# A hybrid decoder block on one core: the diagonal spread in half 0's group norms, row sums on 64 columns, and one value-gate projection moved ahead of v

## The chip, the cores and the metric

The kernel runs on one core of one Trainium2 chip, as one program with one launch. The metric is the device time in microseconds. A core has TensorE (PE, with its weight loads shown as PEld), VectorE (DVE), ScalarE (ACT), GpSimd (POOL) and SyncE (SP), which here issues the DMAs. Each engine works through its own list of instructions in order and waits on semaphores for the others.

## What is computed

One decoder block on x of 1024 tokens by 1024 features, all float32. The tokens are processed in two halves of 512, "half 0" and "half 1".

```python
cond = silu(c) @ ada_w + ada_b                       # shift1, scale1, gate1, shift2, scale2, gate2
h = rmsnorm(x, norm1_g) * (1 + scale1) + shift1
u, v, val, gate = split(h @ w_in + b_in, 4 x 512)    # in order u, v, val, gate
# branch a: causal spatial gating inside chunks of 128 tokens, 8 heads of 64
v = layernorm(gelu(v), a_ln_g, a_ln_b)
y_a = gelu(u) * (tril(w_s) @ v + b_s)
# branch b: gated, causal depthwise convolution of width 31, group norm on 8 groups of 64, swish
y_b = val * sigmoid(gate)
y_b = silu(groupnorm(conv31(y_b) + conv_b))
y = concat(rmsnorm(y_a, out_norm_a_g), rmsnorm(y_b, out_norm_b_g))
x = x + gate1 * (y @ w_out)
h2 = rmsnorm(x, norm2_g) * (1 + scale2) + shift2
g, up = split(h2 @ w_ffn_in, 2)                      # 2 x 2816
x = x + gate2 * ((silu(g) * up) @ w_ffn_out)
return rmsnorm(x, norm_f_g) * (1 + scale_f) + shift_f
```

## The kernel before

Activations lie with features on the 128 partitions and the 512 tokens of a half along the free dimension. So a matrix product is a chain of matmuls of 128 by 128 weights with 512 moving columns into one PSUM bank. To keep float32 accuracy from the rounded format fp32r, each operand is split into a high part (a cast on ScalarE) and a low part (a subtraction on GpSimd or VectorE), and each product is three matmuls: high by high, low by high, high by low (`mm3`, L682 to L684; `product`, L1073).

The block is written as a sequence of stages: first projection of half 0 (value and gate, eight banks at once), `u_proj` of both halves, `v_proj`, `conv`, `spatial`, `a_out` and `b_out`, the value-gate projection of half 1 (`vg_proj(1, ...)`), `w_out`, then the second norm and the feed-forward part. In the feed-forward part twelve "ahead" tiles (`ah`, L1073) are computed before half 1's output projection, eight more after it, and the rest uses a fast product scheme with seven products in place of eight.

The convolution runs on VectorE: 31 taps, each a multiply-add of a shifted row of `ypad` into a PSUM bank `cv` (L1006, L1009, L1011). Of half 0's taps the first six go to ScalarE (L1000) and GpSimd (L1001). Tiles come in pairs (`conv_pair`), and each pair is followed by `group_norm`, which centres two tiles with one matmul each (L1026), squares them (L1029, L1030), sums over groups of 64 partitions in 32-column matmuls (L1033) and forms one 128 by 128 tile of reciprocal standard deviations `gsd` (L1036, L1037). The rows of that tile are then spread back over the partitions of both tiles. There are two ways of doing it:

- by block: 16 matmuls in plain float32 with 64 stationary columns and 128 moving columns, one for each tile, quarter of the tokens and group (L1046). Half 0's group norms do it so.
- from the diagonal: `diagonal` writes the four blocks of 32 rows on the diagonal of a 128 by 512 tile of zeros, each row as a high and a low part (a cast on ScalarE, L617, and four VectorE instructions, L620), and one fp32r matmul for each tile against the selector `late["picks"]` spreads it (L1042). Half 1's group norms and several RMS norms do it so (the set `DIAGONAL`); for these the tile `late` is set up once (`load_late`, L610 to L612), in a buffer that holds the spatial weights `wt` before.

The result is multiplied onto the tile (L1049) and goes through Silu (L1050). `b_out` squares and sums all four tiles (L720, L724, L727), spreads the RMS scale (L730 to L737) and writes `yn_b` (L962) and the high and low parts `y_b` (L964, L965), on which `w_out` (L682 to L684, banks `po`) waits.

`spatial_bias` (L789 to L794) sums each head's causal spatial weights over the source tokens, to carry the layer norm's shift into the bias `bst`: two float32 matmuls of ones with 128 stationary columns and 512 moving ones, and eight VectorE updates of 64 partitions by 128. `v_proj` makes v by tokens, 128 at a time, with Gelu (L910), statistics (L912, L913) and normalisation on VectorE (L921). `glu` writes value times sigmoid of gate into `ypad` (L756, L758).

What is not on the main path is queued as `background`: 24 sums for the conditioning vectors (`ada_cols`) each load 512 KB and multiply and add on VectorE (L636), or on GpSimd and ScalarE (L633, L634); one is issued with each weight or token tile.

The order that runs is not the written order. At the end `fix_order` takes the list of all instructions with their dependencies, estimates durations, computes how long the work behind each instruction is, and lays out each engine's list from that, in several rounds. What the written order does bind is the buffers: tiles of one tag are handed out in the order of the program. The tags that matter here: `w` (eight tiles, the high and low parts of four weights), `raw` (four tiles of 512 KB for loads), `mm` (three PSUM banks), `cv` and `gn` (two banks each), `vn` (four).

## Time and profile before

| | us |
| --- | --- |
| three runs | 966.22, 967.76, 967.87 |
| median | 967.76 |
| the profiled execution, its own time | 967.97 |
| its span (first to last instruction) | 965.9 |
| mean granted TensorE clock | 0.995 of full speed |

The busy times of all engines are on the profile's page, of which the prediction quotes the lines it uses. All rows are of the one profiled execution; times in them count from the start of its span. Rows of a timeline begin with the start and the duration. Float32 matmuls appear as two records for each instruction, fp32r matmuls as one. Consecutive records of TensorE overlap, so what one costs is the distance from its start to the next start.

### The profile page before, as it was taken

How to read it: one execution, taken by the hardware profiler on the slowest of the kernel's cores; microseconds unless marked ns; L12 is line 12 of the kernel's file. 1: busy time of each engine (PE TensorE's matmuls, PEld its weight loads, DVE VectorE, ACT ScalarE, POOL GpSimd, SP SyncE). 2: the span in 40 equal slices, each digit the busy share in tenths (PEclk: the TensorE clock that was granted, in tenths of full speed). 3: DMA queues.
4: the chain of work that ended last, by engine and by line, in shares of the span. 5: the costliest groups of instructions: out<-in, count | busy, mean ns of one | idle time of the engine just before them, and what ended most of it. 6: DMA issues, size and time to landing. Idle time of an engine off the chain costs nothing.

```text
span 965.9 us, 12960 instructions
## 1 busy us (share of the span) xinstructions
PE 950.5 (98%) x4521; PEld 769.6 (80%) x4521; DVE 871.7 (90%) x1236; ACT 474.0 (49%) x756; POOL 408.6 (42%) x241
## 2 busy tenths in 40 slices
PE   8999999999999999999999999999999999999996
PEld 4887777778777778788888888888888888888885
DVE  6999999999999763999999999999879999969956
ACT  5787477643474753564333333333337437227426
POOL 0089988836453413665444444455433100000132
PEclk9999999999999999999999999999999999999998
DMA  9882542343485444844677678867657857415104
GB/s 353 323 310 91 176 152 69 113 174 131 137 282 188 158 136 146 271 173 147 215 245 239 230 237 261 268 211 257 211 177 264 266 172 258 162 33 159 61 1 174
DMA packets 70498, 184.24 MB, mean 191 GB/s; under 512 B 7841, under 2 KB 8353, under 8 KB 70434
## 3 DMA queue, kind: packets, MB, share of 16 engines
q1 hardware_dynamic: 70434, 183.43, 56.5%
q8 instruction: 35, 0.57, 0.2%
q14 instruction: 29, 0.24, 0.1%
HBM read 142.24 MB, written 41.16 MB: 190 GB/s over the span
## 4 chain that ended last, share of the span: by engine, by line
PE 79%; DVE 15%; ACT 2%; DMA 2%; issue 1%; SPq 0%; ACTq 0%; DVEq 0%
PE B L1073 30%; PE C L1073 18%; PE ah L1073 10%; DVE cv L1006 5%; PE A L1073 3%; PE v L682 2%; PE v L684 2%; PE po L682 2%; PE po L684 2%; PE v L683 2%; PE po L683 2%; PE p L684 1%; PE p L683 1%; PE p L682 1%; DVE ada L636 1%
## 5 line engine op out<-in xcount | busy, mean ns | idle before, releaser
L1073 PE MATMUL B<-h,w_f 128*128 128x512 f32 x816 | 189.6, 389 | 0.1
L1073 PEld LDWEIGHTS B<-h,w_f 128*128 128x128 f32 x816 | 153.0, 188 | 32.5 <-ACT x L1291 0.8
L1006 DVE SCALAR_TENSOR_TENSOR cv<-ypad,colt,cv 128x512 f32<-128x512 f32 x216 | 147.0, 744 | 0.2
L1073 PE MATMUL B<-fa,w_d 128*128 128x512 f32 x528 | 124.8, 389 | 0.1
L1073 PE MATMUL C<-h,w_f 128*128 128x512 f32 x528 | 123.4, 389 | 0.0
L1073 PEld LDWEIGHTS B<-fa,w_d 128*128 128x128 f32 x528 | 98.8, 188 | 21.4 <-DVE x L1433 0.7
L1073 PEld LDWEIGHTS C<-h,w_f 128*128 128x128 f32 x528 | 99.1, 188 | 20.6
L1073 PE MATMUL ah<-h,wh_a 128*128 128x512 f32 x320 | 102.4, 396 | 0.3 <-ACT h L699 0.3
L1359 POOL TENSOR_TENSOR sq_nf<-sq_nf,sq_nf 128x512 f32<-128x512 f32 (+1 forms) x15 | 18.0, 1202 | 170.2 <-ACT sq_nf L1353 170.0
L666 POOL TENSOR_TENSOR wl_a<-raw_a,wh_a 128x1024 fp32r<-128x1024 f32 x20 | 49.8, 2488 | 78.2 <-ACT wh_a L665 78.2
L1065 ACT ACTIVATE w_d<-raw_d 128x512 fp32r<-128x512 f32 (+1 forms) x72 | 42.0, 593 | 80.9 <-PE B L1073 32.6
L1065 ACT ACTIVATE w_f<-raw_f 128x512 fp32r<-128x512 f32 x68 | 42.5, 629 | 75.9 <-PE B L1073 41.5
L1316 POOL TENSOR_TENSOR x<-x,up 128x512 f32<-128x512 f32 x20 | 33.2, 1659 | 105.6 <-ACT x L1315 105.6
L1066 DVE TENSOR_TENSOR w_f<-raw_f,w_f 128x512 fp32r<-128x512 f32 x68 | 70.2, 1039 | 2.6 <-ACT w_f L1065 2.5
L1073 PEld LDWEIGHTS ah<-h,wh_a 128*128 128x128 f32 x320 | 60.0, 188 | 15.7 <-ACT h L699 1.4
L1073 PE MATMUL C<-fa,w_d 128*128 128x512 f32 (+1 forms) x291 | 63.9, 370 | 0.0
L1073 PE MATMUL ah<-h,wl_a 128*128 128x512 f32 x160 | 62.5, 390 | 0.0
L1073 PEld LDWEIGHTS C<-fa,w_d 128*128 128x128 f32 x291 | 51.0, 188 | 9.2
L1066 DVE TENSOR_TENSOR fa<-a,fa 128x512 fp32r<-128x512 f32 x77 | 52.4, 720 | 0.4 <-ACT fa L1065 0.4
L1433 DVE SCALAR_TENSOR_TENSOR x<-B,cond,x 128x512 f32<-128x512 f32 x48 | 35.6, 745 | 18.2 <-PE B L1073 18.0
L1066 DVE TENSOR_TENSOR w_d<-raw_d,w_d 128x512 fp32r<-128x512 f32 (+1 forms) x72 | 49.1, 691 | 1.1 <-ACT w_d L1065 1.1
L1065 ACT ACTIVATE fa<-a 128x512 fp32r<-128x512 f32 x77 | 46.1, 625 | 7.1 <-DMA a<-acts 4.0
(265 smaller groups left out, 2111.2 us busy)
## 6 DMA issues: line engine op xcount, KB each, us to landing
acts<-x SPq DMA_DIRECT2D x77, 256.0 KB, 2.9
a<-acts SPq DMA_DIRECT2D x77, 256.0 KB, 4.0
raw_f<-wf SPq DMA_DIRECT2D x32, 512.0 KB, 4.0
ada<-ada SPq DMA_DIRECT2D x24, 512.0 KB, 3.5
x<-ada SPq DMA_DIRECT2D x24, 512.0 KB, 4.4
raw_a<-wf SPq DMA_DIRECT2D x20, 512.0 KB, 3.9
ahead<-ahead SPq DMA_DIRECT2D x40, 256.0 KB, 2.6
ypad<-ada SPq DMA_DIRECT2D x16, 512.0 KB, 5.7
```

What stands on the lines that cost most here:

```text
L636: V.scalar_tensor_tensor(raw, raw, 1.0, cact, op0=ALU.mult, op1=ALU.mult, accum_out=cond[:, j:j + 1])
L666: lo_eng.tensor_tensor(lo[:, cut], raw[:, cut], hi[:, cut].bitcast(F32), op=ALU.subtract)
L682: PE.matmul(acc, shi, mhi, start=start, stop=False)
L683: PE.matmul(acc, slo, mhi, start=False, stop=False)
L684: PE.matmul(acc, shi, mlo, start=False, stop=stop)
L1006: V.scalar_tensor_tensor(accs[j], src, wc, accs[j], op0=ALU.mult, op1=ALU.add)
L1065: A.activation(dst[:, 0, :], src, AF.Copy)
L1066: lo_eng.tensor_tensor(dst[:, 1, :], src, dst[:, 0, :].bitcast(F32), op=ALU.subtract)
L1073: last_mm = PE.matmul(bank[:, cols], s, m[:, cols], start=first and p == 0 and i == 0, stop=p == n - 1 and i == 2, skip_group_check=True)
L1316: G.tensor_tensor(g0, g0, up0, op=ALU.mult)
L1359: G.tensor_tensor(run, run, t, op=ALU.add)
L1433: V.scalar_tensor_tensor(x_tile(k, part), bank[:, cols], ccol(GATE2, k), x_tile(k, part), op0=ALU.mult, op1=ALU.add)
```

## The change

Three things change in the kernel, and a constant tile on the host is built to suit.

1. In `group_norm`, the group norms that are not in `DIAGONAL` (half 0's two) take a fresh tile of 128 by 1024 from the tag `raw`: GpSimd clears its first half, ScalarE widens four columns of a constant into a 128 by 256 selector, and `diagonal` builds the diagonal in it. The 16 float32 matmuls become two of fp32r.
2. `spatial_bias` uses 64 stationary columns: one matmul for the even heads into partitions 0 to 63 and one for the odd heads into 64 to 127 of a single bank, and four VectorE updates on all 128 partitions.
3. `vg_proj(1, (0,))` is written ahead of `v_proj(0)`; tiles 1 and 2 stay where all three were.

```diff
     ("out_norm_a_g", 4), ("out_norm_b_g", 4), ("b_conv_w", 4 * CW),
-    ("sel_grp", 16), ("low_rows", 1), ("sel_hl", 1),
+    ("picks", 4), ("low_rows", 1), ("sel_hl", 1),
...
-    def diagonal(src):
-
-        diag, low = late["diag"], late["low"]
+    def diagonal(src, diag=None, low=None):
+
+        if diag is None:
+            diag, low = late["diag"], late["low"]
         A.activation(low, src, AF.Copy)
...
     def spatial_bias():
-        for q in range(2):
-            rs = mm_bank(f"rs{q}")
-            PE.matmul(rs, ones.broadcast_to([P, P]), wt[:, 4 * q:4 * q + 4, :], start=True, stop=True)
-            for hh in range(4):
-                hd = 4 * q + hh
-                e, hp = hd % 2, hd // 2
-                rows = slice(e * 64, (e + 1) * 64)
-                V.scalar_tensor_tensor(bst[rows, hp, :], rs[rows, hh * P:(hh + 1) * P],
-                                       col("a_ln_b", hp)[rows], bst[rows, hp, :],
-                                       op0=ALU.mult, op1=ALU.add)
+        rs = mm_bank("rs")
+        heads = wt.rearrange("p (a e) t -> p e a t", e=2)
+        for e in range(2):
+            PE.matmul(rs[e * 64:(e + 1) * 64], ones.broadcast_to([P, 64]), heads[:, e], start=True, stop=True)
+        for hp in range(4):
+            V.scalar_tensor_tensor(bst[:, hp, :], rs[:, hp * P:(hp + 1) * P], col("a_ln_b", hp), bst[:, hp, :],
+                                   op0=ALU.mult, op1=ALU.add)
...
         by_block = f"g{half}{jp}" not in DIAGONAL
-        both = sd if by_block else diagonal(sd)
+        picks = None
+        if by_block:
+            both = sb.tile([P, 2 * H], F32R, tag="raw", name=f"gd{half}{jp}", bufs=N_RAW)
+            diag, work = both[:, 0:H], both[:, H:]
+            G.memset(diag.bitcast(F32), 0.0)
+            picks = work[:, P:3 * P]
+            A.activation(picks.rearrange("p (a b) -> p a b", a=4), colt[:, _OFF["picks"]:_OFF["picks"] + 4].unsqueeze(2).broadcast_to([P, 4, 64]), AF.Copy)
+            both = diagonal(sd, diag, work[:, 0:P])
+        else:
+            picks, both = late["picks"], diagonal(sd)
         for i, (j, b) in enumerate(zip(js, (b1, b0))):
-            if not by_block:
-                PE.matmul(b, late["picks"][:, i * P:(i + 1) * P], both, start=True, stop=True)
-            for q in range(4):
-                for g in range(2):
-                    if by_block:
-                        PE.matmul(b[g * 64:(g + 1) * 64, q * P:(q + 1) * P],
-                                  col("sel_grp", 8 * i + 2 * q + g).broadcast_to([P, 64]), sd,
-                                  start=True, stop=True)
+            PE.matmul(b, picks[:, i * P:(i + 1) * P], both, start=True, stop=True)
...
     background += [lambda i=i: ada_cols(SHIFT2 * 8 + i, pool=i < 12) for i in range(16)]
+    vg_proj(1, (0,))
     v_proj(0)
...
-    vg_proj(1, (0, 1, 2))
+    vg_proj(1, (1, 2))
     w_out(0, ya0 + yb0)
```

More of the change, by code (lines that the diff above doesn't have):

```diff
@@ L1536 @@
     gind = np.zeros((P, 34))
-    sel_grp = np.zeros((P, 2, 4, 2))
+    heads = np.zeros((P, 2, 2))
     picks = np.zeros((P, 2 * P + 1))
@@ L1542 @@
             picks[2 * i + g::16, i * P + 64 * g:i * P + 64 * g + 64] = 1.0
-            for q in range(4):
-                sel_grp[32 * q + 2 * i + g, i, q, g] = 1.0
+            heads[2 * i + g::16, i, g] = 1.0
     picks[0::16, 2 * P] = 1.0
-    colv.update(sel_grp=sel_grp.reshape(P, 16),
+    colv.update(picks=heads.reshape(P, 4),
                 low_rows=-(part[:, None] // 16 % 2), sel_hl=((part == 0) | (part == 32))[:, None])
```

## The prediction

> **What bounds the kernel now.** I read the page's first two parts, TensorE's own waits, a table of stages, and then the timelines of single engines around the places that the change touches.
>
> ```profile
> PE 950.5 (98%) x4521; PEld 769.6 (80%) x4521; DVE 871.7 (90%) x1236; ACT 474.0 (49%) x756; POOL 408.6 (42%) x241
> PE   8999999999999999999999999999999999999996
> DVE  6999999999999763999999999999879999969956
> PEclk9999999999999999999999999999999999999998
> ```
>
> TensorE is busy in every slice at the full granted clock, but so is VectorE in the first third. Busy is not the same as never waiting, so next come TensorE's waits between 60 and 400 us (its line, what it waited for, us in total, times, longest):
>
> ```profile
> PE ssq_n L737 <- DVE rt_n L731: 1.0, 1, 1.0
> PE ah L1073 <- ACT h L699: 0.3, 1, 0.3
> PE gn L1026 <- DVE s L1049: 0.2, 1, 0.2
> PE ssq_n L733 <- DVE late L620: 0.2, 1, 0.2
> ```
>
> That is 1.7 us in 340. TensorE is the bound: a microsecond of matmuls taken out is a microsecond of span, as long as what TensorE needs next is also there a microsecond earlier. Whether it is there is VectorE's matter. The table of stages gives the length, then busy us of PE, PEld, DVE, ACT and POOL:
>
> ```profile
> 61.00:212.00 151.00, 150.04 (x863) 118.54 (x862) 150.27 (x218) 100.40 (x150) 123.50 (x70) 1.00 0.43 142
> 266.00:317.00 51.00, 50.68 (x236) 39.61 (x235) 50.61 (x80) 29.17 (x46) 25.28 (x12) 1.00 0.68 233
> 317.00:349.00 32.00, 31.73 (x152) 23.78 (x150) 20.71 (x32) 23.08 (x35) 9.91 (x7) 1.00 0.43 148
> 349.00:966.00 617.00, 607.83 (x2742) 502.24 (x2740) 543.87 (x746) 258.35 (x435) 211.07 (x127) 0.99 0.58 192
> ```
>
> In the two stages up to 317 us VectorE idles 0.7 and 0.4 us: it is as full as TensorE. It first has room from 317 to 349, where 11.3 us are idle. Two engines are full at once, and the change has to be priced on both.
>
> **TensorE: what goes.** The group of the old spread, and rows of TensorE's timeline (start, duration):
>
> ```profile
> L1046 PE MATMUL gn<-gsd,colt x64: 272/273/323, 144.4 to 177.9; 128*64 128x128 f32 x64
> 107.63 1.88 PE L789 MATMUL rs<-wt,ones 128*128 128x512 f32 x4
> 109.29 0.50 PE L682 MATMUL v<-wh_v,h 128*128 128x512 f32 x1
> 144.38 1.97 PE L1046 MATMUL gn<-gsd,colt 128*64 128x128 f32 x32
> 146.28 0.50 PE L684 MATMUL v<-wl_v,h 128*128 128x512 f32 x1
> 319.90 0.39 PE L1042 MATMUL gn<-late 128*128 128x512 f32 x1
> 320.13 0.39 PE L1073 MATMUL ah<-h,wh_a 128*128 128x512 f32 x1
> ```
>
> I count from one start to the next, because the durations overlap. For half 0's first group norm 32 records take 146.28 - 144.38 = 1.90 us; there are 64, so 3.80. Half 1 already spreads from the diagonal: 320.13 - 319.90 = 0.23 for one matmul. Half 0 would need four, 0.92. Saved: 2.9. The full-width matmul behind the narrow block shows 0.50 where others show 0.39, so some 0.1 more for each group norm: 0.2. The row sums: 109.29 - 107.63 = 1.66 us for two matmuls with 128 columns. For 64 columns L1046 is the nearest form: 32 records are 16 matmuls over 128 moving columns in 1.90 us, 0.119 each; two over 512 are eight of those, 0.95. Saved 0.7; the ends are 0 (a narrow one costs as much as a wide one) and 0.83 (exactly half). TensorE's sum: 2.9 + 0.2 + 0.7 = **3.8 us less**, between 3.1 and 3.9.
>
> The Trainium skill (TensorEngine Tiling (Array Packing), section Overview) allows up to twice the speed where the stationary side has 64 columns or fewer. By that rule the row sums would save 0.83 and the sum would be 3.9; the L1046 row stays a little short of it.
>
> **The other engines: what comes.** Rows of their timelines, and one line's group with its shortest, median and longest duration in ns:
>
> ```profile
> 112.51 2.91 DVE L794 SCALAR_TENSOR_TENSOR bst<-rs,colt,bst 64x128 f32<-64x128 f32 x8
> 115.45 2.73 DVE L1006 SCALAR_TENSOR_TENSOR cv<-ypad,colt,cv 128x512 f32<-128x512 f32 x4
> 316.66 1.41 DVE L620 SCALAR_TENSOR_TENSOR late<-late,colt,gsd 32x128 fp32r<-32x128 f32 x4
> 318.10 2.72 DVE L962 SCALAR_TENSOR_TENSOR yn_a<-ya,colt,ssq_a 128x512 f32<-128x512 f32 x4
> 330.22 1.30 POOL L724 TENSOR_TENSOR sq_b<-sq_b,sq_b 128x512 f32<-128x512 f32 x1 [4.60 <-ACT sq_b L720]
> 330.37 2.37 DVE L620 SCALAR_TENSOR_TENSOR late<-late,colt,gsd 32x128 fp32r<-32x128 f32 x4 [0.23 <-ACT late L617]
> 207.24 0.41 ACT L611 ACTIVATE late<-picks_raw 128x257 fp32r<-128x257 f32 x1
> 316.20 0.31 ACT L617 ACTIVATE late<-gsd 128x128 fp32r<-128x128 f32 x1 [1.76 <-DVE gsd L1037]
> 188.61 0.52 POOL L612 MEMSET late<- 128x512 f32 x1
> L921 DVE TENSOR_SCALAR vn<-vn,mv,sd x8: 541/1512/2620, 141.3 to 176.8; 128x512 f32<-128x512 f32 x8
> ```
>
> The bias update falls from eight instructions to four of the same 128 columns on twice the partitions. Eight take 115.45 - 112.51 = 2.94 us, so 1.47 goes; if partitions cost time, less, down to nothing. Each diagonal adds four pieces on VectorE: 318.10 - 316.66 = 1.44 us undisturbed, 2.37 in the other place, where a GpSimd addition ran beside the first piece. Two diagonals are 2.9 to 4.7; I take 2.9, the undisturbed row, as GpSimd is met or not by chance. VectorE's sum: 2.9 - 1.5 = **1.4 us more**, between 1.4 and 4.7.
>
> ScalarE gets for each group norm a cast of the reciprocal (0.31) and the widening of the selector (256 columns; the copy of 257 took 0.41): 1.4 us in all, hidden because ScalarE is busy 100.4 of 151 us in that stage. GpSimd gets two clearings of 0.52, in a stage with 27.5 us idle. In the chain of a group norm, cast and diagonal put 0.31 + 1.44 between reciprocal and spread: the diagonal waits on VectorE, with conv taps (L1006) queued behind it, and the spread waits on TensorE, with the v or value-gate matmuls behind it. Both queues are laid out by the planner, which can put such work ahead, so I cost these waits at nothing; uncovered, they would cost 1.75 us twice.
>
> **What is moved.** The value-gate projection is 48 matmuls, 48 x 0.23 = 11 us of TensorE, the same work in another place: its own price is zero, and half 0's v, its normalisation and spatial mixing come 11 us later. What does that meet? Rows of VectorE, TensorE and ScalarE, and the page's row for the loads of the conditioning sums (KB of one, median us from issue to landing):
>
> ```profile
> 192.73 3.34 DVE L636 SCALAR_TENSOR_TENSOR ada<-ada,cact 128x1024 f32<-128x1024 f32 x1
> 206.45 3.06 DVE L965 TENSOR_TENSOR y_b<-yn_b,y_b 128x512 fp32r<-128x512 f32 x3
> 212.41 0.39 PE L682 MATMUL po<-y_b,wh_o 128*128 128x512 f32 x1
> ada<-ada SPq DMA_DIRECT2D x24, 512.0 KB, 3.5
> 185.56 1.28 ACT L756 ACT_TABLE_LOAD   x1
> ```
>
> Half 0's first normalised conv tile is there at 206.45 + 3.06 / 3 = 207.5, TensorE reads it first at 212.41: 4.9 us to spare, of which the 3.8 faster TensorE and the 1.4 heavier VectorE take 5.2. But ahead of it VectorE does work that is not yet due, such as the reduction of 3.34 us at 192.73, and v's normalisation now comes behind more of conv half 0 than before. I cost this place at nothing. Weights: the projection's four tiles (two weights, high and low) now stand between u's eight and v's eight in a ring of eight, so v's last tiles wait for the projection instead of for u. Today's handover, with v's first matmul at 109.29 right behind the row sums, shows no stall in the waits above; but the row sums, 1.66 us of cover, shrink to 0.95, and if the other 0.7 is bare it costs 0.7. ScalarE's Sigmoid now falls between two runs of Gelu: one or two more table loads of 1.28 us, hidden as above. On SyncE's queue the two weight loads go ahead of v's, and the reductions' loads they carry come earlier; the two diagonals each hold one of four load buffers until their spread.
>
> **Where it ends.** The hard meeting point is half 1's conv branch:
>
> ```profile
> 281.50 0.62 ACT L1030 ACTIVATE s<-gn 128x512 f32<-128x512 f32 x1
> 316.08 0.68 DVE L1006 SCALAR_TENSOR_TENSOR cv<-ypad,colt,cv 128x512 f32<-128x512 f32 x1
> 316.79 0.60 ACT L1017 ACTIVATE s<-cv 128x512 f32<-128x512 f32 x1 [0.28 <-DVE cv L1006]
> 322.08 1.13 PE L1026 MATMUL gn<-s,cstt 128*128 128x512 f32 x2 [0.20 <-DVE s L1049]
> 348.32 1.95 ACT L964 ACTIVATE y_b<-yn_b 128x512 fp32r<-128x512 f32 x3 [3.89 <-DVE yn_b L962]
> 349.10 0.41 PE L682 MATMUL po<-y_b,wh_o 128*128 128x512 f32 x1
> ```
>
> VectorE ends its last conv tap at 316.76 and the copy is done at 317.39. The next matmul on it (L1026) starts only at 322.08, since both banks were still held by the other group norm of half 1: 4.7 us that are no work. From there the chain goes straight on to the first half 1 tile, written from 348.32 to about 348.97, and TensorE reads it at 349.10. Nothing to spare. And TensorE has nothing else then: the same twelve ahead tiles and three banks fill it up to here in both kernels.
>
> So if VectorE ends its taps L us later than now, and the 4.7 us wait can shrink to nothing, the span changes by the larger of -3.8 and L - 4.7. With L = 1.4: L - 4.7 = -3.3. The other group norm of half 1 is ready early enough for that, as its values were copied by 282.12 (the row at 281.50); it was merely put late, in step with TensorE, and with TensorE 3.8 us ahead it moves up by as much: 322.08 - 3.8 = 318.3, beside 317.39 + 1.4 = 318.8. The profiled execution took 967.97 us (span 965.9), 0.21 above the median of 967.76. 967.97 - 3.3 = 964.7, or **964.5** against the median.
>
> **The rivals.** What a measurement of this kernel can tell from no change is about 0.2%, 1.9 us.
>
> First: the wait before L1026 stays 4.7 us, because the planner puts the first group norm of half 1 in step with VectorE's taps, not with TensorE. Then the tap's delay passes through: TensorE waits 3.8 + 1.4 and the span gains 1.4, 969.2. For it: VectorE is as full as TensorE up to 317. Against: the wait is idle time that any earlier place of two short matmuls removes. It reads as no change.
>
> Second, the slower side: the normalisation of v (L921), 11 us later, meets more of GpSimd's work, and so do the diagonals. The eight instructions of L921 run from 0.54 to 2.62 us at one shape, half of them up to 1.51, and the row at 330.37 shows a diagonal stretched by 0.93 beside GpSimd's 1.30. GpSimd is busy 123.5 of 151 us there. If the middle of the eight goes from 1.51 to 2.07, halfway to the longest, that is 8 x 0.56 = 4.5 us; with both diagonals stretched, 1.8 more: L = 1.4 + 6.3 = 7.7, so +3.0, or 970.8 against the median. It decides from L = 6.6 on, where L - 4.7 passes 1.9. Against: they may as well meet less of it, for GpSimd's additions for the conv fall elsewhere too.
>
> The Trainium skill (SBUF — State Buffer, the sections on the port pair that the two engines share) says that a VectorE instruction with two SBUF inputs and a GpSimd one that reads SBUF exclude each other for the whole instruction. The diagonal's pieces are of that kind, and the stretched row agrees.
>
> Third: a diagonal, cleared early, holds a load buffer for long, and a weight arrives late. A load takes 3.5 us from issue to landing (the row above), and one such stall on top of -3.3 gives +0.2, no change: 968.0. Against it: GpSimd can clear late, in 0.52 us.
>
> Fourth, that the order asked for is not the order run: the planner sorts by its own times, and only the order of buffers binds it. That changes no term of the sum, only L.
>
> **How the numbers follow.** The forecast (TensorE's gain less what L eats, so L below 2.8): 0.54. The first rival 0.18, the second 0.22, the third 0.06. Faster by over 0.2% is the forecast: 0.54. Within 0.2%: the first and third rivals, 0.24. Slower: 0.22. The range begins at 963.4 (967.76 - 3.9, and 0.5 for waits of TensorE's 1.7 that may close) and reaches to 970.4, through the first and third rivals and into the second, up to just short of its price. The dearer part of the second rival (0.14) and a forecast that gains more than priced (0.04) lie outside.
>
> **What would show it.** Right: TensorE's records for the spread in half 0 are four of full width, 0.23 from start to start; the row sums take about 0.95; TensorE's waits from 60 to 400 us stay under 3 us; L1026 of half 1's second group norm follows its copy within 2 us; VectorE's last tap ends at 317 to 319. Wrong: a wait of TensorE on y_b or yn_b in half 1, or on h of the second norm, of over 2 us; the last tap beyond 323; L921 with a mean near 2 us; a wait on a weight tile after the moved projection.

## The result, and the profile after

The changed kernel takes 971.86 us (median of 16 runs, 967.26 to 974.14) against 967.38 for the kernel before (16 runs, 965.72 to 968.66): ratio 1.0041 (95% interval 1.0029 to 1.0052). It is slower by 0.4%; the forecast was 964.5.

Line numbers after the change are one or two off those before: L1048 is the spread, L791 the row sums, L919 the normalisation of v, L621 the diagonal's pieces, L1004 a conv tap, L637 a conditioning sum, L738 an RMS spread. Two executions of it are shown below: its profiled one (968.79 us, span 967.0), which is one of its quick ones, and the profiled one of e1, the same kernel once more (span 970.0, nearer to the median).

The page's busy times, first execution:

```profile
PE 947.2 (98%) x4460; PEld 766.2 (79%) x4461; DVE 876.3 (91%) x1240; ACT 474.0 (49%) x760; POOL 409.9 (42%) x243
```

TensorE's work fell by 3.3 us (950.5 before), VectorE's rose by 4.6. Rows of TensorE's timeline (start, duration):

```profile
107.95 1.08 PE L791 MATMUL rs<-wt,ones 128*64 128x512 f32 x4
108.96 0.50 PE L683 MATMUL p<-h,wh_vg 128*128 128x512 f32 x1
157.92 0.62 PE L1048 MATMUL gn<-gd 128*128 128x512 f32 x2
158.38 0.39 PE L684 MATMUL v<-wh_v,h 128*128 128x512 f32 x1
```

The row sums take 1.01 from start to start, the spread 0.23 for each matmul: what was priced. Then TensorE's waits from 60 to 400 us (line, what it waited for, us in total, times, longest), first execution, then e1:

```profile
PE pu L683 <- ACT sg L757: 1.0, 1, 1.0
PE ssq_a L738 <- DVE rt_a L732: 0.9, 1, 0.9
PE po L683 <- ACT y_b L962: 0.9, 1, 0.9
PE gn L1048 <- DVE late L621: 0.8, 1, 0.8
PE gn L1048 <- DVE gd L621: 0.5, 1, 0.5
PE ah L1073 <- DVE ahead L1090: 0.4, 1, 0.4
PE ssq_n L734 <- DVE late L621: 0.2, 1, 0.2
```

```profile
PE pm L945 <- DVE s L1049: 1.7, 1, 1.7
PE ssq_b L738 <- DVE rt_b L732: 1.4, 1, 1.4
```

The kernel before had 1.7 us of waits here. Now there are 4.7 in the quick execution and 7.6 in e1 (these two lines come on top of nearly the same list). The stage tables (length, busy us of PE, PEld, DVE, ACT, POOL), first execution, then the first stage of e1:

```profile
61.00:212.00 151.00, 148.67 (x808) 117.04 (x809) 149.60 (x218) 101.93 (x154) 125.56 (x72) 1.00 0.42 140
266.00:317.00 51.00, 51.00 (x240) 40.54 (x239) 50.56 (x80) 27.19 (x42) 27.60 (x13) 1.00 0.68 218
317.00:349.00 32.00, 30.21 (x141) 21.46 (x139) 26.01 (x38) 22.72 (x35) 9.96 (x7) 1.00 0.36 123
```

```profile
61.00:212.00 151.00, 147.04 (x799) 115.49 (x799) 149.28 (x211) 102.00 (x154) 124.66 (x72) 1.00 0.41 137
```

VectorE is as full as before up to 317 us, and from 317 to 349 it works 26.0 us where it worked 20.7. TensorE now stands still in e1 for 4.0 of these 151 us; before it was 1.0.

For all later comparisons I cut each profiled execution in four by TensorE's timeline: the start of u (first `pu`), from there to the end of half 0's w_out (start of the last `po` of half 0), from there to the first matmul on half 1's `y_b`, and the rest.

| execution | start of u | to the end of w_out, half 0 | to y_b, half 1 | rest | sum |
| --- | --- | --- | --- | --- | --- |
| before | 60.74 | 192.23 | 96.12 | 616.75 | 965.84 |
| after, quick | 61.92 | 189.38 | 97.98 | 617.69 | 966.97 |
| after, e1 | 61.92 | 192.82 | 97.96 | 617.26 | 969.95 |

In the second stage the quick execution does gain 2.85 us, and e1 loses 0.6: the stage is not the same length each time. In the third both lose 1.9. The start is later by 1.2 and the rest longer by 0.5 to 0.9, though nothing in the source was changed there; in e5 and e6, with the same order, u starts at 60.63 and 63.57, so the start varies from one execution to the next.

### The profile page after: what moved, and what is told of

The parts are those of the page before. It is cut to its first block, busy times and chain, and to the rows that moved or that the text cites. A ratio compares the mean times of both kernels' runs of the same rounds, so it can differ in the third digit from the quotient of the medians.

```text
span 967.0 us, 12841 instructions
## 1 busy us (share of the span) xinstructions
PE 947.2 (98%) x4460; PEld 766.2 (79%) x4461; DVE 876.3 (91%) x1240; ACT 474.0 (49%) x760; POOL 409.9 (42%) x243
## 4 chain that ended last, share of the span: by engine, by line
PE 85%; DVE 10%; ACT 2%; DMA 2%; issue 1%; SPq 0%; POOL 0%; ACTq 0%; DVEq 0%; POOLq 0%
PE B L1073 29%; PE C L1073 17%; PE ah L1073 8%; PE A L1073 3%; PE po L683 3%; PE po L685 3%; PE po L684 3%; PE p L683 2%; PE p L685 2%; PE p L684 2%; PE pu L683 2%; PE pu L685 2%; PE pu L684 2%; DVE cv L1004 1%; PE v L685 1%; PE v L684 1%
## 5 line engine op out<-in xcount | busy, mean ns | idle before, releaser
L1004 DVE SCALAR_TENSOR_TENSOR cv<-ypad,colt,cv 128x512 f32<-128x512 f32 x216 | 146.8, 742 | 0.1
```

The lines of the kernel that those rows point to most:

```text
L1004: V.scalar_tensor_tensor(accs[j], src, wc, accs[j], op0=ALU.mult, op1=ALU.add)
```

## The experiments

Times are medians; ratios are against the kernel before on the same chip, with the 95% interval.

### Once more, and each part alone

e1 is the changed kernel, no edit.

> The changed kernel again, for a second profile and a second set of times. All theories: 967 to 974 us as before, median near 971.9, wider than the 3 us of the kernel before. Port theory (VectorE's diagonal pieces collide with GpSimd's conv additions): the last conv tap of half 1 ends at 322 us or later, and a longer execution shows it later still, with TensorE's wait on y_b longer. Plan theory (the order dealt anew leaves TensorE short waits in many places, each decided by how transfers and engines happen to meet): a longer execution shows its extra microseconds in several places, also behind 400 us, in the feed-forward part.

971.9 us, 1.004 (1.0027 to 1.0052). Its third stage is as long as in the quick execution; the second differs by 3.4. Up to 187.5 us the two executions run alike, but for one row at 76.5, and then these rows differ, first of the quick execution and then of e1 (VectorE's last normalisation of v, GpSimd's low part of a weight):

```profile
187.58 0.55 DVE L919 TENSOR_SCALAR vn<-vn,mv,sd 128x512 f32<-128x512 f32 x1
187.72 2.67 POOL L667 TENSOR_TENSOR wl_o<-raw_o,wh_o 128x1024 fp32r<-128x1024 f32 x1 [3.48 <-ACT wh_o L666]
```

```profile
187.56 2.75 DVE L919 TENSOR_SCALAR vn<-vn,mv,sd 128x512 f32<-128x512 f32 x1
187.63 2.39 POOL L667 TENSOR_TENSOR wl_o<-raw_o,wh_o 128x1024 fp32r<-128x1024 f32 x1 [3.40 <-ACT wh_o L666]
```

VectorE's row begins ahead of GpSimd's in both, by 0.14 us in the quick execution, where it takes 0.55, and by 0.07 in e1, where it takes 2.75 and ends 0.29 behind GpSimd's. In e5 and e6 (below, the same order) the lead is 0.01 and 0.09, and it takes 2.69 and 2.76. What follows on VectorE is 2.2 us later in e1. It happens again 20 us on with a conditioning sum (1.22 at 207.00, or 3.43 at 209.19), and the two together make 3.5 us at `rt_b` (210.43 against 213.95) and the 3.4 of this stage. That the runs of this kernel lie between 967 and 974 for this reason is likely, but not shown beyond these executions.

e2 is the kernel before with the projection moved, and nothing else.

```diff
+    vg_proj(1, (0,))
     v_proj(0)
...
-    vg_proj(1, (0, 1, 2))
+    vg_proj(1, (1, 2))
```

> The kernel before with only the value-gate projection moved ahead of v. Port theory: no diagonal is added, so as before within 1 us, 966.5 to 968.5. Move theory (v's normalisation and spatial mixing 11 us later is what makes VectorE late): most of the loss is here, 970 or more. Plan theory: anything within some 4 us of before, with new waits of TensorE that lie elsewhere than in the changed kernel.

969.44, 1.0015 (1.0003 to 1.0027): the move by itself costs some 0.15%, less than the move theory had and more than the port theory.

e3 is the kernel before with half 0's diagonals alone (the parts of the change in `_COLS`, `diagonal`, `group_norm` and the host constants).

> The kernel before with only the diagonal spread in half 0's group norms. Port theory: the whole loss is here: the first diagonal takes 4 us or more instead of 1.4, and the kernel is at 970 or more. Move theory: 2.9 us of TensorE are saved and VectorE gets 2.9 more, so 965 to 967. Plan theory: not told by the sum; new waits of TensorE in places that the diagonal does not touch.

981.57, 1.0123 (1.0101 to 1.0145): by far the worst of the three parts, though it takes 2.9 us of work from TensorE. Its second stage is 199.71 long, 7.5 more than before, and its rest 622.03, 5.2 more, where nothing was added.

e4 is the kernel before with the row sums alone (the change of `spatial_bias`).

> The kernel before with only the row sums on 64 columns. TensorE saves 0.6 to 0.8 us there and VectorE 1.5 us. Port and move theory: 966 to 967, faster by up to 1 us. Plan theory: within some 4 us of before, either way, although both engines got less to do.

969.25, 1.0012 (1.0002 to 1.0022). This one is telling: it takes work away from TensorE (0.65 us) and from VectorE (four instructions) and adds none anywhere, and it got slower, if by little. Its second stage is 194.11 long, 1.9 longer than before. The three parts do not add up either: 0.15, 1.23 and 0.12% alone, 0.4% together.

### Are the diagonals' collisions the cause?

In the changed kernel the diagonals are stretched, as the second rival had it. VectorE's rows of the first diagonal of half 0 and the last one of half 1:

```profile
152.16 5.30 DVE L621 SCALAR_TENSOR_TENSOR gd<-gd,colt,gsd 32x128 fp32r<-32x128 f32 x4
332.70 3.31 DVE L621 SCALAR_TENSOR_TENSOR late<-late,colt,gsd 32x128 fp32r<-32x128 f32 x4 [2.37 <-ACT late L618]
```

5.30 and 3.31 us where 1.44 is the undisturbed time; GpSimd adds conv products without a break from 150.47 to 161.47 beside the first. If VectorE reads the reciprocal from PSUM, its pieces have only one input in SBUF. e5 does that for half 0, with each engine's list written down from the changed kernel, so that the order stays:

```diff
-        V.reciprocal(sd, sd)
+        root, sd = sd, b0[:, P:2 * P] if by_block else sd
+        V.reciprocal(sd, root)
...
-    order, done, follows = forward(g, list(range(len(g.steps))))
...
+    best = None, {e: [g.steps[int(n)] for n in order.split()] for e, order in ORDER.items()}
```

> The changed kernel with its own order of instructions written down, and one operand moved: in half 0's group norms the reciprocal is written into the PSUM bank that the group sums came from, so the diagonal's pieces read one operand from SBUF instead of two. Port theory (the first diagonal's 5.3 us instead of 1.4 decide): four pieces back to 1.4 us in the first group norm, VectorE 3.9 us earlier from 157 us on, 967 to 969 median, and less spread. Plan theory (short waits everywhere, decided by how the engines meet): the pieces shrink, but the time stays above 970, since other instructions meet GpSimd instead.

971.57, 1.005 (1.0037 to 1.0063): nothing gained. Its rows on VectorE and TensorE:

```profile
150.95 1.41 DVE L616 SCALAR_TENSOR_TENSOR gd<-gd,colt,gn 32x128 fp32r<-32x128 f32 x4
```

```profile
156.72 0.62 PE L1044 MATMUL gn<-gd 128*128 128x512 f32 x2
```

The pieces are back at 1.41, done at 152.4; TensorE reads them at 156.7, because that is where its list has them. VectorE then stands still for 3.4 us at its multiplication by the spread norm. Four microseconds were taken from a place where nobody waited. e9 puts all four reciprocals of the group norms into PSUM and lets the planner deal the order anew:

```diff
-        V.reciprocal(sd, sd)
+        root, sd = sd, b0[:, P:2 * P]
+        V.reciprocal(sd, root)
```

> The changed kernel with the reciprocals of all four group norms in PSUM, and the order dealt by the planner for that. TensorE saves its 3.8 us as in the changed kernel, and no diagonal of a group norm can collide with GpSimd. If the diagonals' collisions are the loss: 964 to 967. If the order dealt decides: anywhere from 966 to 975, with waits of TensorE in stage 150 to 215 us that have nothing to do with a diagonal.

970.11, 1.0036 (1.0024 to 1.0048): not the 964 to 967 that it would take if the diagonals' collisions were the loss.

### Is it VectorE's last tap?

The prediction's formula said that half 1 ends by VectorE's taps. e6 and e7 write down the order of the changed kernel and of the kernel before, and take some 8 us of taps away from VectorE in half 1's first pair: 20 taps run over 64 of the 512 columns, so the conv output leaves the other columns out.

```diff
-                    V.scalar_tensor_tensor(accs[j], src, wc, accs[j],
+                    n = 64 if half == 1 and jp == 0 and 10 <= tap < 20 else H
+                    V.scalar_tensor_tensor(accs[j][:, 0:n], src[:, 0:n], wc, accs[j][:, 0:n],
```

> The changed kernel with its own order of instructions written down, but 20 taps of half 1's first conv pair work on 64 columns instead of 512 (the conv output leaves those columns out). VectorE gets some 8 us less to do between 175 and 260 us. If VectorE's lateness at half 1's conv branch is what eats TensorE's 3.8 us: TensorE reads half 1's y_b at 345 to 346 us instead of 349 to 353, and the kernel is at 964 to 968. If the loss lies elsewhere (the stage 150 to 212 or the feed-forward part): less than 2 us are gained, 970 or more.

> The same relief of VectorE by some 8 us (20 taps of half 1's first conv pair on 64 columns, so part of the conv output is left out) in the kernel before with its own order written down. If TensorE is the bound there and VectorE only just keeps up: within 1 us of before. If VectorE is the bound there already: faster by 3 us or more.

e6: 970.91, 1.0041 (1.0029 to 1.0053), third stage 97.96, to the hundredth what it was. e7: 967.36, 1.0001 (0.9992 to 1.0009), third stage 95.84. Where the 8 us went shows in the stage table of e6:

```profile
215.00:266.00 51.00, 49.54 (x240) 39.96 (x239) 42.10 (x81) 18.69 (x26) 25.36 (x13) 1.00 0.45 158
266.00:317.00 51.00, 51.00 (x240) 40.55 (x240) 50.56 (x81) 31.27 (x48) 27.39 (x13) 1.00 0.71 237
```

VectorE stands idle for 8.9 us from 215 to 266 (it had 0.1 there), and is full again behind that. What it waits for there is the residual addition, which needs half 0's w_out:

```profile
DVE x L1057 <- PE po L680: 8.5, 3, 3.9
```

So relief ahead of the end of w_out turns into idle time and does not reach the last tap. It is VectorE's row in the quick execution and in e6:

```profile
321.99 0.75 DVE L1004 SCALAR_TENSOR_TENSOR cv<-ypad,colt,cv 128x512 f32<-128x512 f32 x1
327.08 0.75 DVE L1000 SCALAR_TENSOR_TENSOR cv<-ypad,colt,cv 128x512 f32<-128x512 f32 x1
```

The same points in other executions, from their timelines (e15, e17 and e18 follow below; they keep the order of the kernel before, but for what is said there):

| execution | w_out of half 0 ends | last tap ends | behind w_out by | taps between | y_b of half 1 read | behind the tap by |
| --- | --- | --- | --- | --- | --- | --- |
| before | 252.98 | 316.76 | 63.78 | 61 | 349.10 | 32.34 |
| after, quick | 251.30 | 322.74 | 71.44 | 70 | 349.28 | 26.54 |
| after, e1 | 254.73 | 326.14 | 71.41 | 71 | 352.69 | 26.55 |
| e6 | 256.40 | 327.83 | 71.43 | 70 | 354.36 | 26.53 |
| e15 | 252.23 | 315.73 | 63.50 | 61 | 348.08 | 32.35 |
| e17 | 255.26 | 318.83 | 63.57 | 61 | 351.18 | 32.35 |
| e18 | 252.23 | 320.24 | 68.01 | 64 | 352.59 | 32.35 |

Between the end of w_out and the last tap VectorE is idle for about 1 us or less in each of these. The changed order leaves nine or ten taps more behind w_out, at 0.67 us each, and the last tap comes 7.7 us later after it. From the tap to half 1's `y_b` the distance is fixed in either order, in e18 too, where w_out ends early and the tap does not follow. TensorE is tied to VectorE's list just behind the tap in all of them: it waits 0.2 us for a multiplication by the spread norm in the order of the kernel before, and 0.8 us for the last diagonal in the changed one. So half 1 does end by VectorE's taps, as the prediction had it; e6 shows that what VectorE does ahead of w_out's end does not set them. Relief behind that end was not tried.

### Is it the order?

`fix_order` deals the lists from estimated durations. e8 and e12 change nothing but one of its assumed signal delays, which gives another order for the same work: e8 for the changed kernel, e12 for the kernel before.

```diff
-SIGNAL = {"PE": 0.043, "DVE": 0.024, "Activation": 0.024, "Pool": 0.068, "SP": 0.05}
+SIGNAL = {"PE": 0.044, "DVE": 0.024, "Activation": 0.024, "Pool": 0.068, "SP": 0.05}
```

(e12: DVE 0.030 in place of 0.024.)

> The changed kernel, all operations the same, with one of the planner's constants changed (TensorE's signal time 0.044 instead of 0.043), which deals the order anew in many places. If the operations decide: as the changed kernel, 971 to 973 median. If the order dealt decides: off by 2 us or more to either side, with TensorE's waits in other places.

> The kernel before, all operations the same, with one of the planner's constants changed (VectorE's signal time 0.030 instead of 0.024), which deals the order anew, on VectorE above all. If the order dealt decides by itself: off by 1.5 us or more from before, most likely slower, since the order that was kept is one that ran well. If the order is worth little: within 1 us.

e8: 975.58, 1.0088 (1.0069 to 1.0107). e12: 968.37, 1.0014 (1.0005 to 1.0023). The same work in another order costs the kernel before 0.14%, and takes the changed one from 1.004 to 1.0088. e12 falls between its two expectations.

Two tries to mend the changed kernel's own order by hand. e10 moves one cast on ScalarE behind the high part of y_a, so that GpSimd's subtraction can no longer meet the last normalisation of v; e11 adds the PSUM reciprocals to that.

```diff
-wh_o0_0
...
 y_a0_0
+wh_o0_0
```

> The changed kernel with its own order written down, and one instruction moved by one place on ScalarE: the cast of the first output weight (L666, tile wh_o) stands behind the high part of the first y_a tile instead of ahead of it. GpSimd's subtraction that follows the cast then comes some 2 us later, when VectorE's last normalisation of v is done. Race theory (whether VectorE's normalisation at 187.6 us or GpSimd's subtraction at the same moment starts first costs VectorE 2.2 us, and a second such meeting at 207 us follows from it): the normalisation takes 0.55 us in every execution, the stretch from u's first matmul to the end of the first output projection is 189.5 us or less, the median falls to 967 to 969.5 and the spread to about 3 us. If other things make the changed kernel slow: median still 971 to 973 and spread 4 us or more.

> As the run before, and in all four group norms the reciprocal is written into the PSUM bank of the group sums, so the diagonal's pieces have one SBUF operand. Collision theory for half 1: the last group norm's diagonal takes 1.4 us instead of 3.3, TensorE's wait on its spread (0.8) goes and that on y_b (0.9) shrinks, so the stretch from the end of the first output projection to half 1's first y_b matmul falls from 98.0 to 96.1 to 96.6 us and the kernel is 1.4 to 1.9 us faster than the run before. If that stretch is set by the order alone: 98.0 us as in the four executions so far.

e10: 973.61, 1.0067 (1.0054 to 1.008), a miss. The normalisation takes 0.55 now, but GpSimd's list slid, both conditioning sums ahead of `rt_b` met it (3.4 us each), and TensorE waited 2.8 us at `ssq_b` for `rt_b`. e11: 972.17, 1.0048 (1.0036 to 1.006), third stage 96.86 in place of 97.96, so the collisions of half 1's diagonals account for about 1.1 us in that order (one execution each).

Then the other way round: keep the order of the kernel before, and put the changed work into it. e13 does so for the row sums: two narrow matmuls where the two wide ones stood, four bias updates where the last four of the eight stood, every other instruction where it was. The edit is e4's, and the written-down lists of the kernel before:

```diff
-    order, done, follows = forward(g, list(range(len(g.steps))))
...
+    best = None, {e: [g.steps[int(n)] for n in order.split()] for e, order in ORDER.items()}
```

> The kernel before with only the row sums on 64 columns, as in e4, but every engine's instructions in the order of the kernel before, written down: the two matmuls stand where the two wide ones stood, the four bias updates where the last four of the eight stood. Theory A (the order dealt anew loses what the work gains; e4 was 1.0012 against before): the row sums' 0.7 to 1.0 us now show, u to the end of the first w_out 191.3 to 191.6 instead of 192.23 (e4 194.11), median 966.3 to 966.9. Theory B (VectorE is as full as TensorE, so that TensorE's savings cannot show whatever the order): the stretch stays at 192.1 to 192.4 and the median at 967.2 to 967.7. Worse than 968 would speak against both.

966.26 us, 0.9987 (0.9978 to 0.9996): a gain, from the work that cost 0.12% in e4. The second stage is 190.59 against 194.11 in e4. Of the 1.64 that it is shorter than before, 0.65 are the row sums, and 0.96 a wait of the kernel before's `ssq_n` on `rt_n` that is not there in this execution (nor in e12's, so it may be chance).

e14 adds half 0's diagonals to e13, fitted in by hand: the diagonal and its selector lie in two of the small work tiles and hold no load buffer, the reciprocal is in PSUM, reciprocal and pieces stand ahead of v's normalisation. v stays where it was. e15 puts half 1's reciprocals in PSUM too. e16 is the same two parts dealt by the planner, with the diagonals as the change has them.

```diff
-            both = sb.tile([P, 2 * H], F32R, tag="raw", name=f"gd{half}{jp}", bufs=N_RAW)
-            diag, work = both[:, 0:H], both[:, H:]
+            diag, work = tmp(f"gd{half}{jp}", F32R), tmp(f"gw{half}{jp}", F32R)
...
-        V.reciprocal(sd, sd)
+        root, sd = sd, (b0[:, P:2 * P] if half == 0 else sd)
+        V.reciprocal(sd, root)
```

And e16, against the changed kernel:

```diff
-    vg_proj(1, (0,))
...
-    vg_proj(1, (1, 2))
+    vg_proj(1, (0, 1, 2))
```

> The order of the kernel before, with the row sums as in e13 and half 0's two diagonals fitted in by hand, v's place as before. Each diagonal stands in two of the small work tiles instead of a load buffer, its reciprocal is in PSUM; the reciprocals and pieces are put ahead of the normalisations of v, two conv taps (first group norm) and two short sums of the conditioning (second) behind them. TensorE's work falls by 3.6 to 4.0. Theory A: most of it shows, u to the end of the first w_out 188.5 to 190, the whole 964 to 965.5. If only TensorE's part in the stretch of 61 to 212 us counts and half 1 waits for VectorE's conv taps as before: 965.5 to 967. Theory B: the 1.4 us more on VectorE comes out, 968.5 to 970, the last tap 1.4 to 2 us later and the stretch from there unchanged.

> e14 with the reciprocals of half 1's two group norms in PSUM as well, order unchanged. In e11 against e10 this took 1.1 us from the stretch between the first w_out and half 1's first y_b (97.96 to 96.86). If that comes from the diagonals' pieces no longer meeting GpSimd, it adds here as far as the pieces are on the chain: half 1's last diagonal took 2.37 us in the kernel before and 1.4 undisturbed, so 0.5 to 1.0 off e14. If half 1 is paced by something else: no difference to e14 (within 0.3).

> The change without the moved projection: row sums and half 0's diagonals, dealt by the planner, diagonals in load buffers. The same work as e14 but for the place of the diagonals and of the reciprocal. Theory A: slower than before, 970 to 980, as e3 (the diagonals alone) was at 981.6, while e14 is not. Theory B: like e14, within 2 us.

e14: 968.69, 1.0014 (1.0005 to 1.0024). e15: 967.32, 0.9998 (0.9988 to 1.0008). e16: 978.28, 1.0119 (1.0097 to 1.0142). Between e14 and e16 lie 1.05% (about 10 us) for the same matmuls, by their order, the place of the diagonals and that of the reciprocals. But e14 gains nothing over before either, although TensorE has 3.5 us less to do: the first theory's 964 to 965.5 is a miss. The second had the time (968.5 to 970) but not the place: the last tap ends at 317.12, 0.4 later than before, not 1.4 to 2. And what e15 gains over e14 doesn't lie in half 1's diagonals, as its third stage is 95.85 against 95.95. e14's waits:

```profile
PE pm L940 <- DVE s L1044: 3.5, 3, 1.9
PE pm L940 <- DVE mx L944: 0.6, 1, 0.6
```

The mixing matmuls `pm` of each half's first two tiles use the two `gn` banks, which are free only once VectorE has multiplied by the spread norm. In the kernel before, TensorE spent 1.9 us of each group norm on the narrow spread while VectorE normalised v, and went on to `pm` just as the bank came free. Rows of VectorE and TensorE in the kernel before, whose first narrow spread runs from 144.38 to 146.28, then of TensorE in e14:

```profile
144.10 2.08 DVE L921 TENSOR_SCALAR vn<-vn,mv,sd 128x512 f32<-128x512 f32 x2
146.09 1.27 DVE L1049 TENSOR_TENSOR s<-s,gn 128x512 f32<-128x512 f32 x2
147.17 1.97 PE L947 MATMUL pm<-wt,vn 128*64 128x128 f32 x32
```

```profile
147.05 1.97 PE L940 MATMUL pm<-wt,vn 128*64 128x128 f32 x32 [1.93 <-DVE s L1044]
```

The narrow spread was work that lay beside VectorE's. Taken away, it leaves a wait: `pm` starts at 147.05 in place of 147.17.

### Covering the waits

e17 is e15 with other matmuls put ahead of `pm`: 11 of v before the first two mixing blocks of half 0, 6 between the pairs, 3 and 3 of the value-gate projection in half 1, and VectorE's second multiplication ahead of two other operations.

TensorE's list at the mixing of half 0 (the number of matmuls in brackets):

```diff
-v1_1 (3), pm0_0, pm0_1, v1_1 (5), pm0_2, pm0_3, v1_2 (25)
+v1_1 (8), v1_2 (6), pm0_0, pm0_1, v1_2 (6), pm0_2, pm0_3, v1_2 (13)
```

> e15 with only the order changed at the two places where TensorE waited for VectorE. The mixing matmuls use the banks of the group norm, so they wait until VectorE has multiplied by the spread norm; in the kernel before TensorE spent 1.9 us at each of these places on the narrow spread, beside VectorE's work. Here 11 matmuls of v go ahead of the first two mixing blocks of half 0 and 6 between the pairs, 3 and 3 matmuls of the value-gate projection ahead of the first two blocks of half 1, and VectorE's second multiplication moves ahead of two other operations. Theory A (the spread's work was cover for VectorE, and the gain shows once other matmuls cover it): TensorE's waits from 140 to 215 us fall from 3.9 to under 1, u to the end of the first w_out from 191.31 to 188 to 189, the whole to 964 to 965.5. Rival (VectorE's own work sets the time there, so that the waits only move to another matmul): waits of 3 or more at pm, mx, ssq or y_b, and 966.5 to 968.

970.0, 1.0024 (1.0012 to 1.0037). The waits at `pm` are down to 0.6, and another one is up:

```profile
PE ssq_b L733 <- DVE rt_b L727: 2.5, 1, 2.5
PE gn L1019 <- DVE s L1008: 1.2, 2, 0.8
```

The wait moved on, as the rival had it, though it had a time of 966.5 to 968 and a wait of 3 or more. e18 is e17 with one instruction moved on VectorE, the reciprocal `rt_b`, ahead of six operations that later stages want.

```diff
-ada39, cv1_0, ypad1, cond, cv1_1, cond, cv1_0, rt_b0
+ada39, rt_b0, cv1_0, ypad1, cond, cv1_1, cond, cv1_0
```

> e17 with one instruction moved on VectorE: the reciprocal of half 0's conv-branch norm (rt_b) goes ahead of six operations for work of later stages (three conv taps and a masked gate of half 1, two short sums of the conditioning), all other lists unchanged. Theory (rt_b is where TensorE's lead is given back: its square root was there at 197.9, its reciprocal ran at 202.19 in e17): the wait of ssq_b on rt_b falls from 2.5 to under 0.5 us, u to the end of the first w_out from 195.0 to 191 to 192, the median from 970.0 to 966 to 967.5. Rival (VectorE's work as a whole sets the time, the wait only moves on): a wait of 2 or more at yn_b, y_b or later, and 969 to 970.5.

972.54, 1.0045 (1.0027 to 1.0062), again a miss. `ssq_b` waits no more, w_out begins 4.5 us earlier than in e17 (207.43 against 211.97), and then TensorE waits again, partly behind w_out:

```profile
PE ssq_n L729 <- DVE late L616: 2.2, 1, 2.2
PE ssq_n L723 <- ACT sq_n L716: 1.3, 1, 1.3
PE gn L1019 <- DVE s L1008: 1.2, 2, 0.8
PE po L678 <- DVE ypad L754: 1.2, 1, 1.2
```

Half 0's w_out ends at 252.23, to the hundredth where it ended in e15. The second stage, at 191.58, is as long as the theory had it (191 to 192). But the third is 100.36, 4.4 longer than in e17, as VectorE's last tap does not come earlier with w_out (the table above). In these runs, what TensorE gains ahead of VectorE it gives back at a later place where it needs VectorE.

## Why the prediction was wrong

**TensorE's sum was right.** 3.8 us less were forecast; the row sums saved 0.65 (forecast 0.7), four spreads of 0.23 stand where 3.8 us stood, and the page's busy time fell by 3.3. What went wrong lies in when VectorE has its results ready. Two other signs went against the forecast: TensorE's waits are 4.7 to 7.6 us instead of under 3, and the last tap ends at 322.74 instead of 317 to 319.

**The step that failed is "I cost this place at nothing".** I measured the room at half 0's conv branch between `y_b` (ready at 207.5) and its first matmul (212.41), and found 4.9 us. But TensorE needs the same chain once earlier, when it spreads the branch's RMS scale. Rows of VectorE and TensorE in the kernel before:

```profile
201.55 0.94 DVE L731 RECIPROCAL rt_b<-rt_b 128x128 f32<-128x128 f32 x1
```

```profile
202.59 1.11 PE L737 MATMUL ssq_b<-rt_b,sel_tok 128*128 128x128 f32 x8
```

The reciprocal is done at 202.49 and read at 202.59: 0.1 us to spare, not 4.9. (The working itself took 5.2 us out of the 4.9.) I had quoted VectorE's 150.27 busy of 151 us myself and treated it as room to be arranged. With VectorE full up to that point, TensorE can gain here only what VectorE gains. e1, e10 and e17 wait at this matmul (1.4, 2.8 and 2.5 us), and e14 and e15 at `pm` ahead of it. The quick execution doesn't wait there: its `rt_b` comes 3.5 us ahead of e1's, and its second stage gained 2.85. In the others of that order nothing of the 3.8 is left at the end of w_out: e1's second stage is 0.6 longer than before, not 3.8 shorter.

**The waits of the diagonals were also costed at nothing,** "uncovered, they would cost 1.75 us twice". That the planner would cover them was the mistake: e3 and e16 are 1.2% slower. The old narrow spread had been cover itself (e14), which TensorE's busy time and waits did not show: it counted as bound even where it would otherwise have waited.

**"With L = 1.4" is the term that was wrong in half 1.** The meeting point was the right one, as the fixed distance from the last tap to `y_b` and e18 show. But L, VectorE's delay there, was taken as VectorE's added work, 1.4 us. The last tap came at 322.74, so L was 6.0, and in e1 at 326.14, 9.4. "The larger of -3.8 and L - 4.7" gives +1.3 and +4.7 with these; half 1's first `y_b` was read 0.2 and 3.6 us later than before (349.28 and 352.69 against 349.10), and the spans are 1.1 and 4.1 longer. So the rule holds within 1.1 us, and what it was fed was wrong: the new order leaves nine or ten taps more behind w_out, a cost that the working did not have, and w_out ends 1.7 us earlier in the one and 1.8 later in the other, not 3.8 earlier. The chain behind the tap shrank by 5.8 us, not 4.7. The first rival fell in the changed kernel, though in the runs with the order kept its wait is still there (32.35 from tap to `y_b`). The two rows on TensorE and ScalarE that it is about:

```profile
324.97 1.02 PE L1024 MATMUL gn<-s,cstt 128*128 128x512 f32 x2
```

```profile
324.01 0.57 ACT L1015 ACTIVATE s<-cv 128x512 f32<-128x512 f32 x1
```

The copy is done at 324.58 and the matmul starts 0.4 us later; the 4.7 us of waiting that stood here are gone, as forecast, and the third stage is 1.9 us longer all the same.

**The second rival named the right sign, and a time (970.8) near the result, by a mechanism that only partly holds.** Diagonals were stretched more than it had them (5.30 and 3.31). That v's normalisation would meet more of GpSimd was wrong for the eight together; the groups of before and after on VectorE:

```profile
L921 DVE TENSOR_SCALAR vn<-vn,mv,sd 128x512 f32<-128x512 f32 x8 | 10.7, 1373 | 0.0
```

```profile
L919 DVE TENSOR_SCALAR vn<-vn,mv,sd 128x512 f32<-128x512 f32 x8 | 7.3, 927 | 0.1
```

They met less (9.5 us in e1, still less than 10.7). But the last of the eight, behind which `pm` waits 1.7 us in e1, went from 0.54 (before, at 176.77) to 2.75. And e5 took the stretch out of half 0's diagonals without any gain. What the collisions do explain is the 3.4 us between the two executions, and 1.1 us of half 1 (e11 against e10).

**The fourth rival was waved away: "that changes no term of the sum, only L".** L is the term that decided, and the order by itself moves the time. Every order that the planner dealt anew, for more work or less or the same, was slower than the one before: 1.0012 with less work on both engines (e4), 1.0014 with none changed (e12), 1.0015 (e2), 1.0036 (e9), 1.004 (e1), 1.0088 (e8), 1.0119 (e16), 1.0123 (e3). The row sums alone turn from 1.0012 to 0.9987 when the old order is kept. Against a kept order the change without its move is worth little: the row sums 0.1%, the diagonals nothing (e15).

**What stays open.** e1's loss of 4.1 us in span (start 1.2, second stage 0.6, third 1.8, rest 0.5) is not fully split by cause. That no TensorE saving in the diagonals shows is seen in e14 to e18, and that re-dealing costs in e4, e8 and e12. The runs do not show by which choice the planner came to leave more taps behind w_out, nor why the start varies and the rest is longer. Nor do the runs tell whether the order of the kernel before is an uncommonly good one. The third rival, load buffers held, was not tried by itself; e14 differs from e16 in that too. No wait of TensorE on a weight stands in the lists of the changed kernel above, though, and e9 has one of 1.1 us. e13 is the only version found that beats both kernels.

## What to carry to other kernels

Where two engines are both full, as here, work taken from one shows only if the other is ahead of it at every meeting point. So list all places where the one waits for the other in its list, and take the room at the tightest, not at the last. A kernel whose order is planned by estimates should be changed with the order kept first; then a loss from a new order isn't taken for a loss from the new work.

## What the runs showed of the hardware that was not expected

A wait of TensorE can cost more than itself. Rows of TensorE in e17 after the wait at `ssq_b`:

```profile
203.19 1.64 PE L733 MATMUL ssq_b<-rt_b,sel_tok 128*128 128x128 f32 x8 [2.48 <-DVE rt_b L727]
204.49 0.77 PE L678 MATMUL p<-h,wh_vg 128*128 128x512 f32 x1
205.06 0.63 PE L679 MATMUL p<-h,wl_vg 128*128 128x512 f32 x1
205.49 0.63 PE L680 MATMUL p<-h,wh_vg 128*128 128x512 f32 x1
205.92 0.63 PE L678 MATMUL p<-h,wh_vg 128*128 128x512 f32 x1
...
207.17 0.39 PE L678 MATMUL p<-h,wh_vg 128*128 128x512 f32 x1
207.40 0.40 PE L679 MATMUL p<-h,wl_vg 128*128 128x512 f32 x1
```

The matmuls go at 0.43 from start to start and back to 0.23 only at 207.17; the granted clock is 0.52 from 205 to 207.2 and 1.00 behind that. From `ssq_b` to w_out the same list takes 8.78 us here and 7.05 in e18, 1.7 more. After waits of 1.4 to 1.9 us (e1, e14) the next matmuls go at full speed. Of the nine waits of over 2 us between 60 and 400 us in all these traces, eight were followed by such a stretch, in e18 after 2.16 us and in e16 after 2.29; e3 and e16, the slowest kernels, have four of them. But the length does not decide alone, for the ninth, in e8, was not, and the clock stayed at 1.00:

```profile
188.84 0.50 PE L1048 MATMUL gn<-gd 128*128 128x512 f32 x1 [3.48 <-DVE gd L621]
189.18 0.39 PE L685 MATMUL p<-h,wh_vg 128*128 128x512 f32 x1
189.41 0.39 PE L683 MATMUL p<-h,wh_vg 128*128 128x512 f32 x1
```

The Trainium skill (TensorE: Matmul & The Clock Gate, Part 1) describes such a gate, with half the clock after an idle window of about 3.4 us. Here a wait of 2.16 was enough and one of 3.48 was not, so the measured numbers decide.

The other surprise is how sharp the collision of VectorE and GpSimd is: 0.55 us with a lead of 0.14 us over GpSimd's row, 2.69 to 2.76 with a lead of 0.01 to 0.09 (four executions of one order). The Trainium skill (SBUF — State Buffer, section SBUF: two separate sides) says that whichever starts first has the shared port pair for the whole instruction. The rows of e1 agree that one is held up until the other is done (190.31 and 190.02), but by the starts that the profile records VectorE was first there too, by 0.07 us.
